# Gathered sums two chunks behind their gathers, the prompt's layer 0 finished in the value stage, and the prompt's odd mixers started with the sample's

## The chip, the core and the metric

The kernel runs on one core of a Trainium2 chip. The engines are PE (TensorE, matmuls), DVE (VectorE), ACT (ScalarE), POOL (GpSimd) and SP (SyncE, which issues most DMAs here). Each runs its own instructions in a fixed order and waits for the others by semaphores. The metric is the device time of one execution in microseconds. Before the change the median of three runs is 4570.66 us.

## What is computed

One step of a two-layer trunk on two token groups with the same weights: a prompt of 128 tokens (P) and a sample of 512 (S), of width 1024. Layer 0 mixes with a Fourier transform and a short convolution, layer 1 (the odd one) with an RG-LRU and a bidirectional RWKV-7 scan ("wkv"). After each mixer comes a PEER layer: every token picks 16 of 16384 experts in each of 8 heads, and adds their rows of a table v, weighted by the gelu of its product with their rows of a table u.

```
for l in range(DEPTH):
    sh1, sc1, g1, sh2, sc2, g2 = _modulation(cvec, P['w_mod'][l], P['b_mod'][l])
    h = _layer_norm(x) * (1.0 + sc1) + sh1
    mix = ...                                  # even or odd mixer, then w_out
    x = _layer_norm(ALPHA * x + g1 * mix, P['ln1_g'][l], P['ln1_b'][l])
    h2 = _layer_norm(x) * (1.0 + sc2) + sh2
    ffn = _peer(h2, P['peer_wq'][l], P['peer_keys'][l], P['peer_u'][l], P['peer_v'][l])
    x = _layer_norm(ALPHA * x + g2 * ffn, P['ln2_g'][l], P['ln2_b'][l])

def block(args):                               # inside _peer, by blocks of 128 tokens
    hb, ib, gb = args
    act = jax.nn.gelu(jnp.einsum('td,thkd->thk', hb, u_tab[ib]))
    return jnp.einsum('thk,thkd->td', gb * act, v_tab[ib])
```

## The kernel before

Tokens stand in tiles of 128: the prompt is one tile, the sample is four (0 to 3). The PEER layer is computed in two ways. Tiles 1 to 3 of the sample are dense: all 16384 experts are gone through in 128 chunks of 128, with hidden values from u (`hidden`, L1245), a product with scattered gates (`ge`, L1276) and a matmul with v (L1285). The prompt and tile 0 of the sample are gathered: for each of 128 slots an indirect DMA on POOL brings one row of u or v for each token (`gather`, L1145, 512 KB), and one DVE instruction of 1024 elements either takes its product with h2 (`dot`, L1138) or adds it, weighted, to a sum (`add`, L1166 and L1168). This is 4 x 128 gathers for each of the two layers, 1024 in all; "sum" stands below for either of the two DVE instructions. Names ending in P are the prompt's, in S the sample's.

The gathers are background work. A list of generators (`tasks`) yields once for each gather; `pump(n)` takes n steps, and its callers spread them: each split of a weight tile into two float32r parts pumps `rate` steps (L1225), each pair of one-hot tiles one (L1216), each chunk of the value stage a share of what is left (L1265), and in the odd mixers `pace(n, src)` pumps n steps behind a tiny POOL copy that waits for src (L222). A sum is not issued with its gather: `defer` (L212) keeps two of them back and issues the oldest. The gathered rows go to 4 buffers, and to 3 more in the value stage (`gp`, `gb`).

The stages by time in the profile: even mixers with the prompt's first PEER part to about 420 us; end of layer 0 and routing of the sample, then its gates and half of the early hidden tiles, which go to DRAM (`spill`); the value stage of layer 0 (`dense_peer`, 1023 to 1881), the last norm of the sample's tiles (to 1951); the odd mixers (`odd_mixers`, to 2940); the end of layer 1 (`end`, to 3103); routing heads (to 3415), gates and early hidden tiles (to 3643); the value stage of layer 1 (3643 to 4507) and the last norm.

In layer 0, 88 steps of the prompt's value sum are left over from the value stage (`OVER`, L1375). They run at the start of the odd mixers, paced by the sample's projections. The prompt's own odd mixer waits for them (`while B.tasks`, L1495), then for `peer_out`, and then joins the sample's. The odd mixers' body is `run` (L1378): 16 wkv units of the sample and 4 of the prompt, at most 5 at a time, each a generator, with the RG-LRU beside them; its program order follows from how the generators take turns.

The order in which each engine executes is set when the program is built: the tile framework takes instructions by program order and readiness, so it may move an instruction ahead of one that waits; `issue_after(ins)` keeps the instructions inside it behind ins on its engine. On the chip each engine's order is fixed.

## Time and profile before

| | us |
|---|---|
| median of 3 runs (lowest, highest) | 4570.66 (4562.15, 4586.86) |
| the profiled execution | 4558.22 |
| its span | 4556.4 |
| PE busy | 3837.5 (84%) |
| DVE busy | 3467.4 (76%) |
| POOL busy | 1387.9 (30%) |
| DMA, mean over the span | 263 GB/s |

The shares are means over stages with different limits, so each stage is read by itself: which engine, or DMA, is busy throughout, and what ends the waits of the others. DMA has a mean of 263 GB/s but moves over 340 in several stages and under 130 in others.

### The profile page before, as it was taken

How to read it: one execution, taken by the hardware profiler on the slowest of the kernel's cores; microseconds unless marked ns; L12 is line 12 of the kernel's file. 1: busy time of each engine (PE TensorE's matmuls, PEld its weight loads, DVE VectorE, ACT ScalarE, POOL GpSimd, SP SyncE). 2: the span in 40 equal slices, each digit the busy share in tenths (PEclk: the TensorE clock that was granted, in tenths of full speed). 3: DMA queues.
4: the chain of work that ended last, by engine and by line, in shares of the span. 5: the costliest groups of instructions: out<-in, count | busy, mean ns of one | idle time of the engine just before them, and what ended most of it. 6: DMA issues, size and time to landing. Idle time of an engine off the chain costs nothing. (4 is left out here: it accounts for less than half of the span.)

```text
span 4556.4 us, 71571 instructions
## 1 busy us (share of the span) xinstructions
PE 3837.5 (84%) x26326; PEld 3142.3 (69%) x26326; DVE 3467.4 (76%) x7480; ACT 1757.4 (39%) x3391; POOL 1387.9 (30%) x1105
## 2 busy tenths in 40 slices
PE   7977968999888999778889877719779888988897
PEld 4653767997766788634665654508779877877786
DVE  3398999987889744668554786589999787888845
ACT  2211235763322333244575543203357623332332
POOL 0044322434556200044000232253125354466300
PEclk9997989999999999887888877759999999999999
DMA  9699856999999755368531566487569999999853
GB/s 342 227 350 356 264 196 236 349 357 355 360 360 362 280 175 172 128 237 286 177 101 58 182 222 205 169 289 248 171 225 341 346 367 342 346 365 369 310 170 120
DMA packets 455551, 1198.05 MB, mean 263 GB/s; under 512 B 52848, under 2 KB 195312, under 8 KB 452128
## 3 DMA queue, kind: packets, MB, share of 16 engines
q1 hardware_dynamic: 307744, 656.54, 41.4%
q0 software_dynamic: 147456, 536.94, 32.8%
q8 instruction: 207, 3.39, 0.3%
q14 instruction: 144, 1.18, 0.1%
HBM read 1093.34 MB, written 99.98 MB: 262 GB/s over the span
## 5 line engine op out<-in xcount | busy, mean ns | idle before, releaser
L1079 PE MATMUL ps<-hiS,lwS 128*128 128x384 f32 (+1 forms) x2304 | 817.5, 356 | 81.2 <-DVE lwS L1224 80.9
L1079 PE MATMUL ps<-loS,uhS 128*128 128x384 f32 (+1 forms) x2432 | 857.9, 353 | 1.1 <-DVE loS L432 1.1
L1079 PE MATMUL ps<-hiS,uhS 128*128 128x384 f32 (+1 forms) x2304 | 813.2, 353 | 51.3 <-ACT geS L1252 26.0
L1079 PEld LDWEIGHTS ps<-hiS,lwS 128*128 128x128 f32 x2304 | 447.2, 194 | 111.7 <-DVE lwS L1224 101.4
L1222 ACT ACTIVATE uhS<-w 128x1024 fp32r<-128x1024 f32 x304 | 320.8, 1055 | 527.3 <-PE ps L1079 358.6
L1285 PE MATMUL ps<-vh,ah 128*128 128x512 f32 x1536 | 429.4, 401 | 99.9 <-ACT vh L1222 78.8
L1152 POOL DMA_INDIRECT g<-v,idxP x256 | 351.7, 1374 | 515.8 <-DVE h2P L1168 311.9
L1152 POOL DMA_INDIRECT g<-u,idxS x256 | 349.0, 1363 | 512.9 <-DVE g L1138 391.9
L1079 PEld LDWEIGHTS ps<-hiS,uhS 128*128 128x128 f32 x2304 | 447.5, 194 | 82.3 <-ACT uhS L1222 34.1
L1285 PE MATMUL ps<-lwS,ah 128*128 128x512 f32 x1536 | 483.4, 396 | 10.9 <-DVE lwS L1224 10.8
L1079 PEld LDWEIGHTS ps<-loS,uhS 128*128 128x128 f32 x2432 | 471.5, 194 | 24.0 <-DVE loS L432 3.7
L1285 PE MATMUL ps<-vh,al 128*128 128x512 f32 x1536 | 477.3, 393 | 0.0
L1224 DVE TENSOR_TENSOR lwS<-w,uhS 128x1024 fp32r<-128x1024 f32 x304 | 369.7, 1217 | 122.9 <-ACT uhS L1222 82.0
L1152 POOL DMA_INDIRECT g<-v,idxS x256 | 367.8, 1437 | 237.6 <-DVE h2S L1168 178.6
L1224 DVE TENSOR_TENSOR lwS<-w,vh 128x1024 fp32r<-128x1024 f32 x256 | 312.9, 1223 | 153.7 <-issue 79.3
L1152 POOL DMA_INDIRECT g<-u,idxP x256 | 291.7, 1139 | 414.2 <-DVE g L1138 183.2
L1285 PEld LDWEIGHTS ps<-vh,ah 128*128 128x128 f32 x1536 | 289.1, 192 | 167.1 <-ACT vh L1222 92.5
L1278 ACT ACTIVATE ah<-geS 128x384 fp32r<-128x384 f32 x256 | 134.3, 525 | 671.4 <-PE ps L1285 598.9
L1138 DVE SCALAR_TENSOR_TENSOR g<-g,h2P 128x1024 f32<-128x1024 f32 x256 | 310.2, 1216 | 81.4 <-DMA g<-u,idxP 81.0
L1168 DVE SCALAR_TENSOR_TENSOR h2P<-g,wtP,h2P 128x1024 f32<-128x1024 f32 x254 | 324.6, 1278 | 50.7 <-DMA g<-v,idxP 49.2
L1285 PEld LDWEIGHTS ps<-lwS,ah 128*128 128x128 f32 x1536 | 291.2, 191 | 81.6 <-DVE lwS L1224 20.1
L1285 PEld LDWEIGHTS ps<-vh,al 128*128 128x128 f32 x1536 | 291.4, 190 | 62.8
(480 smaller groups left out, 6687.9 us busy)
## 6 DMA issues: line engine op xcount, KB each, us to landing
w<-ut SPq DMA_DIRECT2D x256, 512.0 KB
w<-v SPq DMA_DIRECT2D x256, 512.0 KB
w<-wblk SPq DMA_DIRECT2D x142, 512.0 KB
w<-wmod SPq DMA_DIRECT2D x96, 512.0 KB
gt<-G SPq DMA_DIRECT2D x64, 768.0 KB
w<-wout SPq DMA_DIRECT2D x56, 512.0 KB
ged<-geS SPq DMA_DIRECT2D x128, 192.0 KB
G<-fa SPq DMA_DIRECT2D x12, 2048.0 KB
```

The lines of the kernel that those rows point to most:

```text
L1079: self.nc.tensor.matmul(out, a[:, s], b[:, k, :], start=k == 0 and i == 0, stop=k == 7 and i == 2)
L1138: self.nc.vector.scalar_tensor_tensor(u, u, 1.0, self.h2[t], OP.mult, OP.mult, accum_out=self.act[t][:, s:s + 1])
L1152: self.nc.gpsimd.indirect_dma_start(out=g, out_offset=None, in_=self.I[tab], in_offset=bass.IndirectOffsetOnAxis(ap=self.idx[t][:, s:s + 1 ...
L1168: nc.vector.scalar_tensor_tensor(acc, v, w[:, s:s + 1], acc, OP.mult, OP.add)
L1222: self.nc.scalar.activation(h, raw, AF.Copy)
L1224: self.nc.vector.tensor_tensor(lo, raw, h.bitcast(F32), op=OP.subtract)
L1278: nc.scalar.activation(ah, ge, AF.Copy)
L1285: nc.tensor.matmul(outs[n][h], a[:, s], b[:, 512 * h:512 * h + 512], start=c == 0 and i == 0, stop=c == 127 and i == 2)
```

## The change

- `defer` keeps back `lag` sums: 2 as before, 5 in the value stages. There the sums of the gathers of one chunk are issued two chunks later, behind that chunk's `al` on DVE (`use_gathered(fresh, i)`).
- In the value stages the gathers of a chunk are issued by `pace` on `ge`: behind a POOL copy that waits for that chunk's gate product. A chunk takes ceil(left / (122 - c)) steps, but at least 2. There are 4 more gather buffers instead of 3, and one more buffer for weight tiles.
- `OVER` is gone. The prompt's value sum and its `peer_out` of layer 0 come first among the tasks, ahead of the sample's, and all is done within the value stage. `rate` in the route is 1 instead of 2.
- The prompt's odd mixer starts at once: `odd_lora`, its RG-LRU and its projections (`wkv_inputs`, now with more turns) take part in `run` from the first turn, and its four wkv units come after the sample's first ones. The pace in the odd mixers is 3 throughout.
- Layer 1's end is new code, `end_tiles`: all four remaining weight tiles of w_out are loaded first, the matmuls of all four token tiles are issued, and then residual, norms and transposes go tile by tile instead of pair by pair.

```diff
@@ -155,7 +155,7 @@
         self.gp, self.gb, self.gn, self.wb, self.wn, self.rp = None, 0, 0, 0, 0, None
-        self.odd, self.tasks, self.pending, self.left = False, [], [], 0
+        self.odd, self.tasks, self.pending, self.left, self.lag = False, [], [], 0, 2
         self.load_constants()
@@ -211,16 +211,16 @@
         self.pending.append(use)
-        self.use_gathered(2)
-
-    def use_gathered(self, left=0):
-        while len(self.pending) > left:
-            f, *a = self.pending.pop(0)
-            with self.later(0):
+        self.use_gathered(self.lag)
+
+    def use_gathered(self, left=0, after=None):
+        with self.tc.issue_after(after.ins) if after else nullcontext():
+            while len(self.pending) > left:
+                f, *a = self.pending.pop(0)
                 f(*a)
...
     def pace(self, n, src):
-        if self.tasks:
+        if n and self.tasks:
             p = self.tl([128, 1], "pace", 2)
@@ -374,13 +374,13 @@
 
-    def row_of(self, src):
-        o = self.B.wide("row", 3)
+    def row_of(self, src, bufs=3):
+        o = self.B.wide("row", bufs)
         self.nc.sync.dma_start(o, src.broadcast_to([128, D]))
...
 
-    def mrow(self, l, v):
-        return self.row_of(self.B.md[l, v][self.row:self.row + 1, :])
+    def mrow(self, l, v, bufs=3):
+        return self.row_of(self.B.md[l, v][self.row:self.row + 1, :], bufs)
 
@@ -504,6 +504,48 @@
         self.todo.append((grp, pts))
+
+    def end_tiles(self, l, hT, lo):
+        nc, B = self.nc, self.B
+        ws = []
+        for k in range(self.early, 8):
+            w = B.rp.tile([128, D], F32, name=B.name("wo"), tag="wo", bufs=8 - self.early)
+            nc.sync.dma_start(w, self.I["wout"][l, k])
+            ws.append(w)
+        self.end_load(l)
+        xs = []
+        for t in range(self.nt):
+            x = self.tmp()
+            nc.sync.dma_start(x, self.x[t])
+            xs.append(x)
+            if t == 1:
+                break
+        g1 = self.mrow(l, 2, 5)
+        g, b = self.row_of(self.I["lnaff"][l, 0:1], 5), self.row_of(self.I["lnaff"][l, 1:2], 5)
+        mc = self.mcols(l, 3)
+        self.h2, self.todo, pts = {}, None, []
+        for t in range(self.nt):
+            pts.append([self.pst(*(("pB", 2) if t == 3 else ())) for _ in range(2)])
+            for k in range(self.early, 8):
+                for h in range(2):
+                    nc.tensor.matmul(pts[t][h], self.yT[:, k, t * 128:(t + 1) * 128],
+                                     ws[k - self.early][:, 512 * h:512 * h + 512], start=k == self.early, stop=k == 7)
+        for t in range(self.nt):
+            if t < len(xs):
+                x = xs[t]
+            else:
+                x = self.tmp()
+                nc.sync.dma_start(x, self.x[t])
+            self.residual(x, pts[t], g1, 1.0)
+            self.norm([x], g, b)
+            self.save(t, x)
+            self.norm([x])
+            self.transposed([x], (t,), mc, hT, lo)
+            if t not in self.dense:
+                sh2, sc2 = self.mrow(l, 3, 5), self.mrow(l, 4, 5)
+                h2 = self.h2[t] = self.keep([128, D], "h2")
+                nc.vector.scalar_tensor_tensor(h2, sc2, 1.0, x, OP.add, OP.mult)
+                nc.vector.tensor_tensor(h2, h2, sh2, op=OP.add)
 
@@ -616,6 +658,7 @@
             lo.append(o)
+            yield
         nc.scalar.activation(lo[0], lo[0], AF.Tanh)
@@ -733,6 +776,8 @@
                     self.shift(z[:, hp, :], z[:, hp, 1:T + 1], 4 * i + hp)
+                    if hp < 3:
+                        yield
                 rkv.append([z[:, 0:2, 1:T + 1], z[:, 2:4, 1:T + 1]])
@@ -1257,12 +1302,10 @@
         f.update(zip(self.dense, outs))
+        self.B.lag, fresh = 5, 0
         for c in range(128):
...
                 self.B.finish_task(first)
-            elif c < LAST:
-                more = self.B.left - (OVER if l < DEPTH - 1 else 0)
-                self.B.pump(max(0, -(-more // (LAST - c))))
             if 0 not in f and first not in self.B.tasks:
@@ -1276,7 +1319,14 @@
             nc.scalar.activation(ah, ge, AF.Copy)
-            nc.vector.tensor_tensor(al, ge, ah.bitcast(F32), op=OP.subtract)
+            i = nc.vector.tensor_tensor(al, ge, ah.bitcast(F32), op=OP.subtract)
+            if self.B.lag > 2:
+                self.B.use_gathered(fresh, i)
+            had = len(self.B.pending)
+            if c < LAST:
+                more = self.B.left
+                self.B.pace(min(more, max(2, -(-more // (LAST - c)))), ge)
+            fresh = max(0, len(self.B.pending) - had)
             vh, vl = self.split(self.dt, "vh", self.I["v"][l * NEXP + c * 128:l * NEXP + (c + 1) * 128])
@@ -1327,20 +1377,24 @@
             with B.tc.tile_pool(name=f"ends{l}", bufs=1, reuse_waits="tile") as B.rp:
-                self.end(l, self.hi, self.lo, l == 0 and (lambda: B.modulation(1, 0)))
+                if self.early:
+                    self.end_tiles(l, self.hi, self.lo)
+                else:
+                    self.end(l, self.hi, self.lo, l == 0 and (lambda: B.modulation(1, 0)))
             B.rp = None
...
                 self.peer_tiles(l)
-                B.rate = 2
+                B.rate = 1
+                if l == 0:
+                    B.add(P.values(0))
+                    B.add(P.peer_out(0), n=1)
                 for h in self.route(l, self.groups[0]):
...
                 B.add(self.dots(0, range(128)), mine, n=256)
-                if l == 0:
-                    B.add(P.values(0))
                 self.spilled = {}
@@ -1354,10 +1408,10 @@
             with B.tc.tile_pool(name=f"dense{l}", bufs=1, reuse_waits="tile") as self.dense_pool:
-                B.gp, B.gb, B.rp = self.dense_pool, 3, self.dense_pool
+                B.gp, B.gb, B.wb, B.rp = self.dense_pool, 4, 1, self.dense_pool
                 B.rate, f = 0, {}
                 self.dense_peer(l, G, ges, mine, f)
-                B.gp, B.gb = None, 0
+                B.gp, B.gb, B.wb, B.lag = None, 0, 0, 2
                 for grp in (((1, 2), (3,)), ((1,), (2,), (3,)), ((1,), (2, 3)))[1]:
@@ -1372,7 +1426,7 @@
 SPILL = 16
-LAST, OVER = 122, 88
+LAST = 122
 
@@ -1492,16 +1546,11 @@
     def prompt(own, side):
-        while B.tasks:
-            yield
-        for _ in range(4):
-            yield
-        yield from P.peer_out(l - 1)
-        B.odd_rate = 3
-        P.odd_lora(l)
+        yield from P.odd_lora(l)
         lru, wkv = [P.odd_lru(l, c) for c in range(4)], list(P.odd_wkv(l))
...
         side[n:n] = lru
+        yield from P.wkv_inputs(l, P.inputs, 0)
         own.extend(wkv)
@@ -1517,9 +1566,10 @@
 
-    B.odd, B.odd_rate = True, 6
+    B.odd, B.odd_rate = True, 3
     B.odd_constants()
-    S.odd_lora(l)
+    for _ in S.odd_lora(l):
+        pass
     lru = [S.odd_lru(l, c) for c in range(4)]
```

How many sums (of 1024) stand on DVE in each stretch of its order, between instructions that both kernels have:

| stretch of DVE's order | before | after |
|---|---|---|
| up to the sample's first top-k of layer 0 | 78 | 78 |
| its routing heads | 74 | 67 |
| gates and early hidden tiles | 63 | 17 |
| value stage of layer 0, first to last gate product | 209 | 348 |
| then to the last wkv output | 184 | 157 |
| end of layer 1, to the sample's first top-k | 59 | 92 |
| its routing heads | 43 | 5 |
| gates and early hidden tiles | 58 | 0 |
| value stage of layer 1 and behind | 256 | 260 |

In the row that ends with the last wkv output, the 184 are 88 value sums of layer 0 and 96 dots of layer 1, the 157 are 2 value sums of the sample's tile 0, the prompt's 128 dots and 27 of its value sums. In the end of layer 1, 59 are 32 dots and 27 value sums, and the 92 are value sums alone.

Place one is POOL's order in the value stage of layer 0 (g are gathered rows, `pace` the copy that waits for a chunk's gate product `geS`). Before:

```order
L1152 DMA g_10816<-v,idxS_2899 128x1024
L1152 DMA g_10852<-v,idxS_2899 128x1024
L1152 DMA g_10855<-v,idxS_2899 128x1024
L1152 DMA g_10889<-v,idxS_2899 128x1024
L1152 DMA g_10892<-v,idxS_2899 128x1024
```

After:

```order
L1197 DMA g_11445<-u,idxS_2899 128x1024
L225 COPY pace_11515<-geS_11305 128x1
L225 COPY pace_11589<-geS_11347 128x1
L1197 DMA g_11447<-u,idxS_2899 128x1024
L1197 DMA g_11517<-u,idxS_2899 128x1024
L225 COPY pace_11661<-geS_11389 128x1
L1197 DMA g_11519<-u,idxS_2899 128x1024
```

The gathers stood in one row without a copy between them, each held only by its buffer; now they stand in groups behind a copy from the gate product.

Place two is DVE's order in the same stage (`lwS` is the low part of a split weight tile, `al` that of the gated hidden values). Before:

```order
L1279 TENSOR_TENSOR al_10862<-geS_10646,ah_10861 128x384
L1168 SCALAR_TENSOR_TENSOR h2S_8844<-g_10813,wtS_8841,h2S_8844 128x1024
L1168 SCALAR_TENSOR_TENSOR h2S_8844<-g_10816,wtS_8841,h2S_8844 128x1024
L1224 TENSOR_TENSOR lwS_10869<-w_10865,vh_10867 128x1024
L1279 TENSOR_TENSOR al_10899<-geS_10714,ah_10898 128x384
L1168 SCALAR_TENSOR_TENSOR h2S_8844<-g_10852,wtS_8841,h2S_8844 128x1024
L1276 TENSOR_TENSOR geS_10821<-geS_10821,gt_10969 128x384
L1276 TENSOR_TENSOR geS_10858<-geS_10858,gt_10969 128x384
```

After:

```order
L1269 TENSOR_TENSOR lwS_10905<-w_10901,vh_10903 128x1024
L1183 SCALAR_TENSOR_TENSOR g_10852,actS_2900<-g_10852,h2S_2756 128x1024
L1322 TENSOR_TENSOR al_10929<-geS_10724,ah_10928 128x384
L1269 TENSOR_TENSOR lwS_10947<-w_10943,vh_10945 128x1024
L1183 SCALAR_TENSOR_TENSOR g_10854,actS_2900<-g_10854,h2S_2756 128x1024
L1322 TENSOR_TENSOR al_10971<-geS_10797,ah_10970 128x384
L1183 SCALAR_TENSOR_TENSOR g_10856,actS_2900<-g_10856,h2S_2756 128x1024
L1319 TENSOR_TENSOR geS_10841<-geS_10841,gt_11009 128x384
L1269 TENSOR_TENSOR lwS_10989<-w_10985,vh_10987 128x1024
```

Sums stood wherever they fitted in; now they stand behind the `al` of a later chunk, here dots of the sample's tile 0, where the kernel before has come to its value sums.

Place three is DVE's order in the end of layer 1, in the second norm of the first token tiles (`rsS` is the norm's small state, `h2P` the prompt's sum). Before:

```order
L1138 SCALAR_TENSOR_TENSOR g_26917,actP_21590<-g_26917,h2P_21528 128x1024
L401 TENSOR_SCALAR rsS_26525<-mvS_26524 128x2
L402 TENSOR_SCALAR rsS_26525<-rsS_26525 128x2
L403 TENSOR_SCALAR rsS_26525<-rsS_26525 128x2
L405 TENSOR_TENSOR rsS_26525<-rsS_26525 128x2
L1138 SCALAR_TENSOR_TENSOR g_26953,actP_21590<-g_26953,h2P_21528 128x1024
L406 SCALAR_TENSOR_TENSOR rsS_26525<-rsS_26525 128x2
L407 SCALAR_TENSOR_TENSOR rsS_26525<-rsS_26525 128x2
L405 TENSOR_TENSOR rsS_26525<-rsS_26525 128x2
L406 SCALAR_TENSOR_TENSOR rsS_26525<-rsS_26525 128x2
```

After:

```order
L1213 SCALAR_TENSOR_TENSOR h2P_27566<-g_30048,wtP_27563,h2P_27566 128x1024
L405 TENSOR_TENSOR rsS_26746<-rsS_26746 128x1
L405 TENSOR_TENSOR rsS_26826<-rsS_26826 128x1
L1213 SCALAR_TENSOR_TENSOR h2P_27566<-g_30109,wtP_27563,h2P_27566 128x1024
L406 SCALAR_TENSOR_TENSOR rsS_26746<-rsS_26746 128x1
L406 SCALAR_TENSOR_TENSOR rsS_26826<-rsS_26826 128x1
L1213 SCALAR_TENSOR_TENSOR h2P_27566<-g_30136,wtP_27563,h2P_27566 128x1024
L407 SCALAR_TENSOR_TENSOR rsS_26746<-rsS_26746 128x1
L407 SCALAR_TENSOR_TENSOR rsS_26826<-rsS_26826 128x1
L1213 SCALAR_TENSOR_TENSOR h2P_27566<-g_30158,wtP_27563,h2P_27566 128x1024
```

Before, one dot stands between nine small steps; now a value sum stands between each small step and the next, two tiles' steps being paired.

## Rows read from the trace of the kernel before

**Rows 1.** Busy time of each engine by stage: window, length, busy (instructions), granted clock, DMA.
```profile
core 0: us, PE busy (x) PEld busy (x) DVE busy (x) ACT busy (x) POOL busy (x), PEclk, DMA share, GB/s
1023.00:1881.00 858.00, 783.93 (x3658) 670.29 (x3659) 607.94 (x726) 274.58 (x371) 282.81 (x204) 0.98 0.80 286
3643.00:4507.00 864.00, 789.23 (x3634) 683.38 (x3635) 659.21 (x857) 272.18 (x365) 355.02 (x252) 0.96 0.87 312
...
2940.00:3103.00 163.00, 60.11 (x199) 36.14 (x198) 125.83 (x223) 21.14 (x40) 80.73 (x67) 0.67 0.84 289
3103.00:3415.00 312.00, 264.04 (x1391) 239.53 (x1390) 308.80 (x1117) 133.73 (x272) 56.99 (x44) 0.94 0.61 206
...
3415.00:3643.00 228.00, 216.75 (x1429) 216.17 (x1427) 192.57 (x169) 163.16 (x404) 102.67 (x59) 0.99 0.94 344
```

**Rows 2.** The same view of three stretches of the value stages.
```profile
1202.00:1530.00 328.00, 269.42 (x1204) 220.79 (x1203) 289.75 (x317) 88.85 (x120) 194.64 (x140) 0.97 0.98 361
1585.00:1785.00 200.00, 200.00 (x973) 176.19 (x972) 94.13 (x117) 73.90 (x101) 0.00 (x0) 1.00 0.55 177
3880.00:3981.00 101.00, 100.01 (x484) 87.82 (x483) 84.42 (x125) 36.26 (x50) 41.90 (x35) 1.00 0.97 348
```

**Rows 3.** The same stretches, the gate product (L1276, one a chunk) alone.
```profile
1202.00:1530.00 328.00, 21.70 (x40) 0.97 0.98 361
1585.00:1785.00 200.00, 17.62 (x32) 1.00 0.55 177
3880.00:3981.00 101.00, 8.89 (x16) 1.00 0.97 348
```

**Rows 4.** The page's DMA queue of the gathers: packets, MB, share of 16 engines.
```profile
q0 software_dynamic: 147456, 536.94, 32.8%
```

**Rows 5.** Busy time of each engine in six stretches of the odd stage.
```profile
1951.00:2029.00 78.00, 63.59 (x158) 28.79 (x156) 55.61 (x78) 29.95 (x54) 41.49 (x41) 0.94 0.80 277
2029.00:2114.00 85.00, 66.96 (x906) 38.23 (x906) 76.40 (x161) 54.27 (x105) 37.09 (x36) 0.76 0.78 258
2114.00:2228.00 114.00, 82.66 (x1163) 61.61 (x1162) 84.14 (x211) 41.96 (x96) 31.10 (x28) 0.66 0.71 243
2228.00:2536.00 308.00, 270.18 (x4403) 193.11 (x4406) 161.56 (x534) 205.23 (x452) 0.67 (x4) 0.85 0.31 97
2536.00:2839.00 303.00, 240.26 (x3329) 168.26 (x3320) 235.70 (x721) 125.71 (x269) 90.38 (x112) 0.77 0.63 212
2839.00:2940.00 101.00, 82.33 (x1359) 65.89 (x1360) 62.32 (x206) 26.03 (x67) 20.82 (x28) 0.67 0.42 143
```

**Rows 6.** Groups of DVE in 1068:1537: busy us, mean ns; idle before, releaser.
```profile
L1168 DVE SCALAR_TENSOR_TENSOR h2S<-g,wtS,h2S 128x1024 f32<-128x1024 f32 x127 | 162.8, 1282 | 1.8
L1224 DVE TENSOR_TENSOR lwS<-w,vh 128x1024 fp32r<-128x1024 f32 x62 | 75.5, 1220 | 6.2 <-ACT vh L1222 6.2
...
L1279 DVE TENSOR_TENSOR al<-geS,ah 128x384 fp32r<-128x384 f32 x62 | 34.2, 552 | 9.6 <-ACT ah L1278 9.6
```

**Rows 7.** All gathers (L1152): time from issue to landing.
```profile
DMA to landing us min/median/max: 4.1/7.3/14.6
```

**Rows 8.** Waits in 1068:1537: who waited for whom, total us, times, longest.
```profile
POOL g L1152 <- DVE h2S L1168: 96.7, 75, 8.3
```

**Rows 9.** The POOL copies of L225 from the odd units, ns min/median/max.
```profile
L225 POOL COPY pace<-e x12: 181/619/1102, 2037.1 to 2853.4; 128x1 f32<-128x1 f32 x12
```

**Rows 10.** Waits in 2550:2930: who waited for whom.
```profile
DVE g L1138 <- DMA g<-u,idxP: 53.9, 35, 8.3
```

**Rows 11.** Groups of DVE in 2940:3103, the end of layer 1.
```profile
L1138 DVE SCALAR_TENSOR_TENSOR g<-g,h2P 128x1024 f32<-128x1024 f32 x32 | 38.8, 1214 | 9.5 <-DMA g<-u,idxP 9.3
L1168 DVE SCALAR_TENSOR_TENSOR h2P<-g,wtP,h2P 128x1024 f32<-128x1024 f32 x26 | 33.4, 1284 | 8.9 <-DMA g<-v,idxP 8.7
...
L552 DVE TENSOR_TENSOR half<-ps,row 128x512 f32<-128x512 f32 x8 | 5.4, 682 | 17.5 <-DMA w<-wout 17.5
```

## The prediction

> **What bounds the kernel now.** I read the stages first, by the busy time of the engines in each [rows 1], then the inside of each stage. The two value stages (layer 0 from 1023 to 1881 us, layer 1 from 3643 to 4507) have two regimes, shown by three stretches [rows 2], in which the gate product, once a chunk, counts the chunks [rows 3]. In 1202:1530 there are 40 chunks in 328 us and 140 gathers (all of POOL's instructions there), the DMA engines are 0.98 busy at 361 GB/s, and PE idles. In 1585:1785 there are 32 chunks in 200 us and no gather, PE is busy throughout and DMA moves 177 GB/s. In 3880:3981 there are 16 chunks in 101 us with 35 gathers: PE is busy throughout and DMA moves 348 GB/s. So a chunk costs PE 6.25 us (200/32) and DMA 1.106 MB (177 GB/s x 200 us / 32), and a gather 0.524 MB (537 MB over the program's 1024 [rows 4]). Three and a half gathers a chunk need (1.106 + 3.5 x 0.524) / 0.361 = 8.15 us of DMA, and 8.2 was measured; two need 5.97 us, less than PE wants. **Two gathers a chunk are free, each further one costs 1.45 us.** DVE comes close behind: in the DMA-bound regime it works for 290 of 328 us.
>
> The odd stage (1951 to 2940) is read in six stretches [rows 5]. [...] In 2228:2536, with no sum, PE is busy for 270 of 308 us at 0.85. The last two stretches hold 96 of the prompt's dots. Layer 1's end up to the first top-k of the sample (2940:3103) belongs to DVE, 126 of 163 us, while PE works for 60. The routing heads behind it (3103:3415) are DVE's alone, 309 of 312 us. The gates and early hidden tiles (3415:3643) are PE's, 217 of 228 us [rows 1].
>
> **The change part by part**, against the profiled execution (4558 us, span 4556). Where the sums stand in DVE's order is the table ahead of this.
>
> Value stage of layer 0. It now takes 348 sums where it had 209: the 88 that were left to the odd stage, and those that one pump instead of two for each split leaves behind in the route. The pace gives three gathers a chunk while more than two are left for each remaining chunk, so 106 chunks with three, 16 with two, 6 with none. 106 x (1.106 + 3 x 0.524) / 0.361 = 787 us, 22 x 6.25 = 138, together 924 us against 858: **+66**. Lower bound: all bytes at the ceiling without a gap, (128 x 1.106 + 348 x 0.524) / 0.361 = 897, +39. Upper bound: three gathers cost what 3.5 cost in the row, 8.2 us, 106 x 8.2 + 138 = 1007, +149. I stand by the first, since bytes explain both regimes. DVE needs 3 x 1.28 for the sums, 1.22 for v's split, half of that for u's (half of the tiles come from the spill), 0.55 twice [rows 6]: 6.8 us of 7.4, so it follows, with little to spare. The sum stands two chunks (14.8 us) behind its gather, which lands within 14.6 us at worst, 7.3 by the median [rows 7]; eight buffers and the issue of three gathers hold this, and POOL's present waits for a sum to free a buffer [rows 8] move to the pace. The prompt's last norm, inside the stage, is covered by DMA.
>
> A pace copy reads SBUF on POOL while DVE's sums read two SBUF operands. The row of such copies gives 181, 619 and 1102 ns as least, median and largest [rows 9], so some wait for something; POOL, with 3 gathers in 7.4 us, has room for that. [...]
>
> Value stage of layer 1. 258 sums at nearly two a chunk: 14 chunks with three, 14 x 7.42 = 104 us, and 114 at 101/16 = 6.31, 720 us; 824 against 864: **-41**. Bounds: 128 x 6.25 = 800 (-64), and no change (0) if the spacing costs what the idle DMA of its last 222 us gave.
>
> Routing heads. DVE-bound, so a sum taken out is worth its time: in layer 1 the count falls from 43 to 5, 38 x 1.27 = 48, less a little because PE's own 264 us come near: **-45** (-48 to -30). In layer 0 it falls by 7: **-8**. The sums that leave the gates' stretch (58 and 46) lay under a PE that was 95% busy: 0, and they now cost where they land.
>
> Odd stage. Without its 88 sums the first 277 us could run as 2228:2536 does: 213 us of PE at 270/308 are 243, -34; and 83 us of it at 0.85 instead of 0.66 are 64, -19. That includes the prompt's projections, which move ahead of the first units. Together -55 (0 to -90). The late part gets 155 sums where it has 96, because the prompt's dots end earlier and 27 value sums follow them before the last units are out. 59 x 1.28 = 76 us of DVE work, and by now the dots' own waits for their gathers take 54 us [rows 10]. Against that, the prompt's top-k starts after the 11th of 20 units instead of the 14th: three units more of cover, 3 x 33 us (308 us for 9 units) at a DVE that is idle for 48%, 48 us, and the stretch itself has another 20 us or so. I take +10 (-20 to +110, that is the 76 plus 59 x 0.56 of waits). Sum **-45** (-110 to +55).
>
> End of layer 1. 92 sums stand between its steps, where 59 did (58 of them in the window of [rows 11]), one after nearly every small operation of the norms. DVE's work: 126 - 39 - 33 = 54 for the end itself, 92 x 1.28 = 118 for the sums. The wait of 17.5 us at its start [rows 11] remains, with 7 sums (9 us) in it. 54 + 118 + 8.5 = 180 against 163, +17 with no wait for a gather; with the present 0.31 us for each sum (9.3 + 8.7 over 58) 209, +46. The tiles' own pipeline (all four weights first, tile by tile on DVE) gives something back: **+33** (+15 to +60).
>
> Tails. The last gathers are now summed in the last chunks, so tile 0 is finished behind them instead of far earlier: four half-row steps and two of statistics at 0.68 us [rows 11], two at 1.28 and some small ones, 8 to 9 us of DVE, half of it beside the last chunks' matmuls: **+4** for each layer, +8 (0 to +17).
>
> Sum: 66 - 41 - 45 - 8 - 45 + 33 + 8 = -32: 4526 us in the profile's terms.
>
> **Rivals.** (a) The odd stage packs densely: once no sum stands in its first half, PE stays near the 88% of the free stretch to the end and the clock stays up. Odd stage -110 instead of -45, end +17: 4526 - 65 - 16 = 4445. For it: clock and busy share rise together in the rows. Against: 155 sums in its second half. [...] (b) Slower: the value stage of layer 0 saturates both DMA and DVE. DVE executes in order; if a sum's gather is late even by half a microsecond at 361 GB/s, the split behind it is late, PE waits, and the next pace with it. Then a chunk with three gathers costs the 8.2 us of [rows 2]: +149 instead of +66, 4609. It decides from about 7.7 us a chunk, where 106 x 0.3 = 32 us have eaten the gain. For it: DVE at 6.8 of 7.4 us. Against: in the DMA-bound regime DVE waited for gathers hardly at all (1.8 us beside 127 sums [rows 6]). (c) Four buffers feed the 92 and 27 sums around layer 1's end, and DVE stands behind each: odd stage -10, end +60, 4526 + 35 + 27 = 4588. (d) The pacing doesn't do what it says: layer 1's value stage keeps its 864 us, 4567.
>
> **How the numbers follow.** A measurement of this kernel can tell about 0.5% (23 us) from no change. Forecast 0.42 (own range 4490 to 4560, so 0.26 faster and 0.16 within); (a) 0.25, faster; (b) 0.18, slower; (c) 0.11, slower; (d) 0.04, within. That makes faster 0.51, within 0.20, slower 0.29. The median of the runs shown, 4570.66, lies 0.27% above the profiled execution, 12 us: 4526 becomes 4538. The range takes in (a) with most of its spread and (b) likewise: 4425 to 4640; outside stay an odd stage at its lower bound with everything else well, and (b) together with (c). The signs share the cases: the forecast's own range is 4502 to 4572.
>
> **What would show it.** Right: layer 0's value stage 900 to 940 us long with DMA near 360 GB/s to its last chunks; layer 1's 810 to 835 with PE busy nearly throughout; a first wkv unit without sums around it and a clock over 0.8 in the odd stage's first half; an end of layer 1 of 180 to 210 us; heads of layer 1 in some 265 us. Wrong: DVE waits for gathers in the value stages, layer 0 over 960 us, or an odd stage as long as before (989 us) because its second half has become DVE's.

## The result

The changed kernel takes 4501.1 us (median of 4 runs, 4496.9 to 4510.8) against 4572.2 us of the kernel before in the same session (4562.2 to 4586.9): a ratio of 0.9845 with a 95% interval of 0.9813 to 0.9877, 71 us faster. The forecast was 4538, and faster; the range held the time, but the gain is twice the one forecast.

Of the 71 us the two traces show 55 (spans 4556 and 4501 us); the other 16 are the profiled executions, of which that of before was a quick one (4558 beside a median of 4572) and that of after was not. By the markers that the prediction used (first and last gate product, first and last unit, first top-k), in us:

| stage | before | after | change | forecast |
|---|---|---|---|---|
| start to first sample top-k, layer 0 | 456 | 460 | +4 | 0 |
| routing heads, layer 0 | 348 | 338 | -10 | -8 |
| gates, layer 0 | 219 | 216 | -3 | 0 |
| **value stage, layer 0** | 854 | 894 | **+40** | +66 |
| last gate product to 11th unit | 547 | 466 | **-81** | -55 +4 |
| 11th unit to last wkv output | 516 | 570 | **+54** | +10 |
| end of layer 1 | 162 | 215 | **+53** | +33 |
| routing heads, layer 1 | 312 | 262 | -50 | -45 |
| gates, layer 1 | 228 | 236 | +8 | 0 |
| **value stage, layer 1** | 864 | 797 | **-66** | -41 |
| last chunk to the end | 46 | 43 | -3 | +4 |

The busy time by stage of the kernel after answers [rows 1]; the columns are those of [rows 1].

```profile
core 0: us, PE busy (x) PEld busy (x) DVE busy (x) ACT busy (x) POOL busy (x), PEclk, DMA share, GB/s
1014.00:1908.00 894.00, 794.79 (x3654) 681.77 (x3655) 765.59 (x951) 272.26 (x371) 560.87 (x470) 0.96 0.98 360
3657.00:4454.00 797.00, 764.38 (x3644) 668.92 (x3645) 646.43 (x842) 272.48 (x369) 453.41 (x380) 0.98 0.96 344
2943.00:3159.00 216.00, 62.33 (x195) 38.73 (x196) 171.67 (x291) 24.89 (x65) 117.72 (x93) 0.62 0.82 280
3159.00:3421.00 262.00, 238.85 (x1326) 219.36 (x1325) 260.08 (x1078) 127.99 (x265) 3.75 (x4) 0.98 0.48 160
3421.00:3657.00 236.00, 228.66 (x1500) 228.28 (x1498) 122.97 (x109) 166.44 (x408) 0.00 (x0) 0.99 0.57 201
```

The value stage of layer 1 is now PE's, 764 of 797 us. In the end of layer 1 (2943:3159) DVE works 172 us where it worked 126, beside a PE that is no busier than it was. The gates of layer 1 behind the heads (3421:3657) have no POOL instruction left, and DMA falls from 0.94 to 0.57: room that nobody uses. Inside the value stages, two stretches answer [rows 2], and the gate products in them (L1319 now) answer [rows 3]:

```profile
1304.00:1760.00 456.00, 412.39 (x1909) 353.77 (x1907) 399.05 (x533) 139.53 (x190) 313.40 (x258) 0.97 1.00 373
3872.00:4169.00 297.00, 297.00 (x1439) 262.10 (x1438) 241.78 (x326) 105.71 (x144) 162.19 (x139) 1.00 0.95 341
...
1304.00:1760.00 456.00, 35.12 (x65) 0.97 1.00 373
3872.00:4169.00 297.00, 26.57 (x49) 1.00 0.95 341
```

The windows begin and end with a gate product, so that 65 of them are 64 chunks. In layer 0 these take 456 us, 7.1 us each, with 193 gathers and DMA at 1.00 and 373 GB/s, which is more than the 361 of [rows 2]. In layer 1, 48 chunks take 297 us, 6.2 each, with 93 gathers and PE busy throughout.

Just ahead of the first of these stretches stands the prompt's last norm of layer 0. Its eight chunks took 79 us with 24 gathers, where other groups of eight with 22 to 26 gathers took 52 to 60, and DMA fell to 309 GB/s. The second line is from the waits in 1225:1760: POOL's copy waited for gate products, once for 27.2 us. In every kernel below in which the prompt ends early, the group with this norm is the longest of layer 0, 74 to 134 us. No run took the norm out of the stage.

```profile
1225.00:1304.00 79.00, 59.80 (x257) 49.16 (x256) 67.28 (x109) 22.16 (x31) 38.45 (x32) 0.87 0.86 309
...
POOL pace L225 <- DVE geS L1319: 37.5, 12, 27.2
```

The odd stage in three stretches (before: [rows 5]): no gather in the first, 139 POOL instructions in the second, and a clock of 0.54 in the last, where PE works for 72 of 125 us.

```profile
2047.00:2374.00 327.00, 286.71 (x4779) 198.72 (x4778) 175.33 (x570) 217.54 (x485) 0.00 (x0) 0.86 0.36 113
2374.00:2818.00 444.00, 364.22 (x4990) 250.33 (x4988) 350.50 (x1070) 202.19 (x428) 126.93 (x139) 0.79 0.61 202
2818.00:2943.00 125.00, 71.60 (x1281) 57.82 (x1280) 84.83 (x163) 27.22 (x64) 58.44 (x56) 0.54 0.68 228
```

### The profile page after: what moved, and what is told of

It is laid out like the page before. It is cut to its first block, busy times and chain, and to the rows that moved or that the text cites. A ratio compares the mean times of both kernels' runs of the same rounds, so it can differ in the third digit from the quotient of the medians.

```text
span 4501.2 us, 72085 instructions
## 1 busy us (share of the span) xinstructions
PE 3794.0 (84%) x26326; PEld 3122.6 (69%) x26326; DVE 3463.1 (77%) x7548; ACT 1749.2 (39%) x3413; POOL 1534.8 (34%) x1317
## 5 line engine op out<-in xcount | busy, mean ns | idle before, releaser
L1124 PE MATMUL ps<-hiS,lwS 128*128 128x384 f32 (+1 forms) x2304 | 807.8, 352 | 53.0 <-DVE lwS L1269 52.7
L1335 PE MATMUL ps<-vh,ah 128*128 128x512 f32 x1536 | 411.0, 397 | 66.9 <-ACT vh L1267 59.3
L1197 POOL DMA_INDIRECT g<-v,idxS x256 | 385.1, 1504 | 238.6 <-DVE h2S L1213 192.2
L1197 POOL DMA_INDIRECT g<-v,idxP x256 | 337.7, 1319 | 359.8 <-DVE h2P L1213 194.7
L225 POOL COPY pace<-geS 128x1 f32<-128x1 f32 x244 | 149.2, 616 | 748.4 <-DVE geS L1319 704.0
```

The costliest lines, as they stand in the source:

```text
L225: self.pump(n, self.nc.gpsimd.tensor_copy(p, src[:, 0:1]))
L1124: self.nc.tensor.matmul(out, a[:, s], b[:, k, :], start=k == 0 and i == 0, stop=k == 7 and i == 2)
L1197: self.nc.gpsimd.indirect_dma_start(out=g, out_offset=None, in_=self.I[tab], in_offset=bass.IndirectOffsetOnAxis(ap=self.idx[t][:, s:s + 1 ...
L1335: nc.tensor.matmul(outs[n][h], a[:, s], b[:, 512 * h:512 * h + 512], start=c == 0 and i == 0, stop=c == 127 and i == 2)
```

## The experiments

The change is three things at once: how gathers and sums are handed out in the value stages (distance, pace, buffers), the prompt's early end of layer 0, and the new end of layer 1. My theory after the two traces: the first part carries the gain, because sums five behind and held in place make the gathers even, and the prompt's early end loses on one side (end of layer 1, layer 0's value stage) what it brings on the other. The rivals: the gain comes from the odd stage being clear, or within the first part from the buffers or the pace alone. Stages in the table are in us, by the markers above; odd is from the last gate product to the last wkv output.

| kernel | median, ratio to before (95%) | value 0 | odd | end 1 | heads 1 | gates 1 | value 1 |
|---|---|---|---|---|---|---|---|
| before | 4572 | 854 | 1063 | 162 | 312 | 228 | 864 |
| after | 4501, 0.9845 (0.9813 to 0.9877) | 894 | 1035 | 215 | 262 | 236 | 797 |
| value stages alone | 4490, 0.9817 (0.9792 to 0.9841) | 823 | 1072 | 165 | 318 | 215 | 812 |
| after, old buffers | 4538, 0.9916 (0.9888 to 0.9944) | 924 | 1035 | 216 | 262 | 235 | 806 |
| after, two behind | 4506, 0.9850 (0.9824 to 0.9875) | 896 | 1037 | 217 | 263 | 241 | 790 |
| after, no pace | 4495, 0.9827 (0.9802 to 0.9852) | 887 | 1031 | 217 | 267 | 238 | 787 |
| after, pace only | 4541, 0.9922 (0.9894 to 0.9950) | 929 | 1037 | 216 | 263 | 240 | 793 |
| after, neither holds | 4583, 1.0021 (1.0006 to 1.0035) | 894 | 1055 | 212 | 333 | 215 | 801 |
| after, four a chunk | 4596, 1.0053 (1.0034 to 1.0071) | 925 | 1033 | 212 | 262 | 237 | 859 |
| values held | **4415**, 0.9650 (0.9621 to 0.9680) | 896 | 1011 | 99 | 331 | 227 | 794 |
| held, old end | 4433, 0.9687 (0.9662 to 0.9711) | 894 | 1006 | 114 | 334 | 228 | 786 |
| held, value stages alone | 4492, 0.9818 (0.9800 to 0.9837) | 818 | 1072 | 120 | 345 | 233 | 824 |
| held in both layers | 4418, 0.9650 (0.9619 to 0.9680) | 889 | 995 | 100 | 331 | 233 | 803 |
| held, two in gates | **4370**, 0.9551 (0.9528 to 0.9573) | 848 | 1014 | 100 | 331 | 234 | 790 |

### The value stages alone

The kernel before with the new hand-over (from defer's lag to pace on ge, fourth gather buffer, wide buffer); everything else old. Of its diff, the hand-over and the buffers:

```diff
-            elif c < LAST:
-                more = self.B.left - (OVER if l < DEPTH - 1 else 0)
-                self.B.pump(max(0, -(-more // (LAST - c))))
...
+            if c < LAST:
+                more = max(0, self.B.left - (OVER if l < DEPTH - 1 else 0))
+                if more:
+                    self.B.pace(min(more, max(2, -(-more // (LAST - c)))), ge)
...
-                B.gp, B.gb, B.rp = self.dense_pool, 3, self.dense_pool
+                B.gp, B.gb, B.wb, B.rp = self.dense_pool, 4, 1, self.dense_pool
```

> The kernel before with the new way of handing out gathers in the value stages alone: sums queued five behind and placed behind the rounding error, the POOL copy that waits for ge, a fourth gather buffer and a wide one. 88 gathers of the prompt are still held back, the prompt still ends layer 0 inside the odd stage, and end, odd stage and routing rate are those of before. Theory A, that this part carries the gain and that the early prompt costs about what it gives back: the value stage of layer 1 falls from 864 to about 798 us as in the changed kernel, that of layer 0, which has 139 sums fewer than the changed kernel's 348, falls from 854 to about 800, and heads, odd stage and the end of layer 1 stay within 10 us of before; 4572 - 66 - 54 is about 4450, faster than the changed kernel's 4501. Theory B, that the gain comes from the order as a whole (the prompt's last work out of the odd stage) and that the value stage of layer 0 gains nothing without it: about 4572 - 66, 4505.

4490 us. Layer 1's stage gained 52 and layer 0's 31, not 54; no other stage moved by more than 13. This part alone gives 82 us, no less than the whole change (the two intervals overlap), so the early prompt and the new end together gave nothing that can be measured, as they stand. Theory A is right in its claim, 40 us too hopeful in its sum.

### Distance, pace, buffers

> The changed kernel with three extra gather buffers and no extra wide one in the value stages, as before. Theory A, that the gain of the value stages rests on sums that stand far enough behind their gathers, and that six gathers open at a time need the buffers: a gather waits for the buffer of the sum it follows, and the two value stages lose 20 to 60 us together, 4521 to 4561. Theory B, that the pace and the place of the sums are enough: within 10 us of 4501.

```diff
-                B.gp, B.gb, B.wb, B.rp = self.dense_pool, 4, 1, self.dense_pool
+                B.gp, B.gb, B.wb, B.rp = self.dense_pool, 3, 0, self.dense_pool
```

4538, theory A's figure: 30 us of it in layer 0's stage, 8 in layer 1's. Its reason, that five queued sums need the buffers, is put to the test by the run with the pace alone.

> The changed kernel with sums queued two behind their gathers in the value stages, as before, and not placed behind the rounding error; the POOL copy that waits for ge, the buffers and all else are the changed kernel's. Theory A, that DVE's wait for a gather's rows is what the stage of layer 1 lost before, and that the distance takes it away: the stage of layer 1 goes back from 798 us to 850 or more and that of layer 0 from 894 to 940 or more, 4600 in all. Theory B, that the even pace alone takes it away: within 15 us of 4501.

```diff
-        self.B.lag, fresh = 5, 0
+        self.B.lag, fresh = 2, 0
```

4506, theory B: the distance that gave the change its name, and the place behind `al` that the kernel uses only with it, are worth nothing that can be measured while the pace is there.

> The changed kernel without the POOL copy that waits for ge in the value stages: gathers are handed out in the same numbers, at least two per chunk, but nothing ties their issue to the chunk. Sums stay five behind, and the buffers are the new ones. Theory A, after the run in which sums stood only two behind and the time stayed at 4506: the pace is what the value stages gain from, and without it both lose what they had gained, value stage of layer 1 from 798 to about 850 us, of layer 0 from 894 to about 940, 4600 in all. Theory B, that any of the three (pace, distance, buffers) is enough where the other two stay: within 15 us of 4501.

```diff
-                self.B.pace(min(more, max(2, -(-more // (LAST - c)))), ge)
+                self.B.pump(min(more, max(2, -(-more // (LAST - c)))))
```

4495, theory B again: neither is the pace, while the distance is there. The stages are 7 and 10 us shorter without its copies, which the intervals of the two kernels don't tell apart.

> The changed kernel with sums two behind and the gather buffers of before in the value stages, so that only the pace is left of that part. Its order has 64 sums of layer 1's dots in heads and gates, 58 less in the value stage. Theory A, that buffers count only because five queued sums hold them (the run with the old buffers and five behind lost 30 us in layer 0's value stage and 8 in layer 1's): with two behind they are enough, 4501 within 15 us. Theory B, that fewer buffers cost by themselves, because gathers land late: 4530 to 4560.

```diff
-        self.B.lag, fresh = 5, 0
+        self.B.lag, fresh = 2, 0
...
-                B.gp, B.gb, B.wb, B.rp = self.dense_pool, 4, 1, self.dense_pool
+                B.gp, B.gb, B.wb, B.rp = self.dense_pool, 3, 0, self.dense_pool
```

The order that this text speaks of is not that of this kernel; its heads and gates have 7 and 0 sums, where the changed kernel's have 5 and 0. 4541, theory B for layer 0, where the fewer buffers cost 35 us with two sums queued, as they cost 30 with five; in layer 1 nothing is lost (793). This kernel's whole stage and its middle, windows and gate products as in [rows 2] and [rows 3], beside the 894 and 456 us above:

```profile
1011.00:1940.00 929.00, 809.63 (x3640) 686.23 (x3641) 770.73 (x967) 272.36 (x369) 571.41 (x470) 0.95 0.94 345
1303.00:1789.00 486.00, 422.09 (x1916) 358.43 (x1915) 407.62 (x539) 139.65 (x190) 329.28 (x266) 0.96 0.97 357
...
1303.00:1789.00 486.00, 34.53 (x64) 0.96 0.97 357
```

Here the windows' ends fall just outside two gate products, and 64 chunks take 486 us. Six gathers more (199 for 193) are by estimate some 8 of the 30 us, at 0.524 MB each [rows 4] and 373 GB/s; the rest is DMA, which moves 357 GB/s where it moved 373. Over the whole stage, with the same 348 gathers, it is 345 for 360. Where three gathers a chunk make DMA the bound, these buffers are bandwidth. The gather buffer and the one for weight tiles were always taken away together, so which of them counts is not shown.

So buffers explain that loss in layer 0, and the gain in layer 1 survived the loss of each of the three. What is left is what all these kernels share. Counted per eight chunks of layer 1 in the traces (gathers issued, us), first group to last:

```
before      us  31 57 76 53 50 50 50 61 65 65 65 57 50 50 50 35
       gathers   8 28 29 17 17 16 17 29 28 28 28  7  0  0  0  0
after       us  50 58 57 50 50 50 50 48 51 49 49 51 50 48 51 38
       gathers  18 23 21 15 16 16 16 16 15 13 18 17 13 18 17  6
```

The last group ends with the last gate product and is seven chunks. Eight chunks take 50 us with 0 gathers and with 16, 57 with 23, 65 with 28 (57 and 76 in the two groups of the first pack, 67 on average). Before, gathers ran ahead of the chunk that handed them out, in two packs at 28, and the last four groups had none. Two runs put this to the test, each able to fail.

> The changed kernel with one number changed: at least four gathers handed out per chunk in the value stages for at least two; pace, distance and buffers are the changed kernel's. In its order the value stage of layer 1 has 21 to 25 sums in each of ten groups of eight chunks and then hardly any, where the changed kernel has 16 in nearly all. Theory A, that evenness is what the value stage of layer 1 gained: eight chunks take 50 us with up to 16 gathers, 57 with 24 (the changed kernel's groups in layer 0), 65 with 28 (before), so 798 us becomes about 850, layer 0 stays within 15 us of 894, and the whole takes about 4555. Theory B, that the stage's time goes by the sum of gathers, however they lie, or by the waits that distance and buffers took away: within 15 us of 4501.

```diff
-                self.B.pace(min(more, max(2, -(-more // (LAST - c)))), ge)
+                self.B.pace(min(more, max(4, -(-more // (LAST - c)))), ge)
```

Theory A in layer 1: 859 us for the stage, with distance, pace and buffers in place; 4596 in all, half a per cent slower than before the change, where theory A had 4555. The trace has 18 to 25 gathers in each of the first eleven groups of layer 1, about three a chunk, then 2, then none. The windows of a stretch with gathers and of the one behind it, without, and their gate products:

```profile
3731.00:4133.00 402.00, 364.05 (x1669) 314.82 (x1669) 349.52 (x493) 121.92 (x166) 259.68 (x222) 0.96 1.01 375
4358.00:4507.00 149.00, 149.00 (x723) 131.57 (x722) 69.29 (x85) 54.28 (x72) 0.00 (x0) 1.00 0.53 175
...
3731.00:4133.00 402.00, 30.86 (x57) 0.96 1.01 375
4358.00:4507.00 149.00, 13.25 (x25) 1.00 0.53 175
```

First 56 chunks at 7.2 us with DMA full and PE waiting, then 24 at 6.2 with DMA half idle: what the first stretch loses, the second can't give back, since PE has its own floor. Layer 0 lost 31 us too, which theory A had not said: its pack of 67 gathers in the fourth group, where the prompt's last norm stands, took 134 us, and the last two groups had none.

> The changed kernel without either of the two things that tie gathers to the chunk (the POOL copy that waits for ge, and sums placed behind the rounding error, five behind); the new buffers and the numbers handed out stay. Alone, each of the two could be taken out at no cost (4495 and 4506 us). In the order 64 sums of layer 1's dots move ahead into its heads (58 sums for 5) and gates (13 for 0), and its value stage has 24 in each of four groups of eight chunks and none in the last five. Theory A, that either of the two is enough to keep gathers where they are handed out, and that without both they run ahead: heads 262 to about 335, value stage 798 to about 815, 4580 in all. Theory B, that the buffers carry the gain: 4501 within 15 us.

```diff
-        self.B.lag, fresh = 5, 0
+        self.B.lag, fresh = 2, 0
...
-                self.B.pace(min(more, max(2, -(-more // (LAST - c)))), ge)
+                self.B.pump(min(more, max(2, -(-more // (LAST - c)))))
```

Theory A: 4583. Without both, heads and gates hold 66 sums more and the value stage 64 fewer; it is no shorter (801, with PE busy for 764), for PE's floor of 6.2 us a chunk is there, and the heads pay 71 us for 53 sums. With the gates, which are 21 us shorter, that is 50 us for 66 sums; another 20 lie in the odd stage, which holds as many sums as it did (155 for 157), and why it is longer no run shows. The heads' window and the stage's:

```profile
3175.00:3508.00 333.00, 279.21 (x1480) 254.75 (x1479) 330.28 (x1189) 136.94 (x278) 76.02 (x59) 0.94 0.66 226
3723.00:4525.00 802.00, 764.01 (x3635) 665.57 (x3636) 592.95 (x735) 272.26 (x367) 248.11 (x186) 0.99 0.83 296
```

DVE is busy for 330 of the 333 us of the heads. So the pace, and the sums placed behind the rounding error, are two locks on one door: either keeps the gathers where the chunk hands them out.

### The sums in the end of layer 1

The end of layer 1 was the largest loss. Its groups on DVE and who DVE waited for, in the kernel after (before: [rows 11]):

```profile
L1213 DVE SCALAR_TENSOR_TENSOR h2P<-g,wtP,h2P 128x1024 f32<-128x1024 f32 x93 | 119.3, 1283 | 37.4 <-DMA g<-v,idxP 37.2
...
L594 DVE TENSOR_TENSOR half<-ps,row 128x512 f32<-128x512 f32 x8 | 5.4, 682 | 6.6 <-DMA row<-md 6.6
```

93 value sums for 119 us, and 37 us of waits for their gathers, in a stage of 216.

> The changed kernel with one line changed: in layer 1 the hand-over of one gather per weight tile in the routing goes through a small POOL copy that reads that tile, so that the 92 value sums of the prompt that now stand in the end of layer 1 (3 are left there) fall into its heads (51) and gates (61, none before). Theory A, that the end of layer 1 grew from 162 to 215 us because these sums and their gathers stand between its few DVE instructions, and that the gates, where TensorE is busy 229 of 236 us, take them free: end 216 to about 115, heads 262 to about 310 (before had 43 sums there and took 312), gates 236 to 240, 4501 - 50, about 4450. Theory B, that the end is held by its own chain and by its loads, and the sums only fill its waits: end 216 to about 200, heads plus 50, 4530.

```diff
-        self.B.pump(self.B.rate)
+        (self.B.pace if self.B.odd else lambda n, _: self.B.pump(n))(self.B.rate, raw)
```

Theory A, and more of it than I had asked for: 4415. The windows of the end, the heads, the gates:

```profile
2920.00:3020.00 100.00, 60.59 (x200) 38.85 (x201) 64.51 (x205) 25.99 (x68) 4.97 (x8) 0.76 0.38 137
3020.00:3350.00 330.00, 266.93 (x1383) 242.07 (x1383) 317.82 (x1126) 131.85 (x269) 83.85 (x94) 0.90 0.60 208
3350.00:3578.00 228.00, 218.08 (x1437) 217.50 (x1435) 193.10 (x168) 161.42 (x402) 115.37 (x99) 0.99 0.93 345
```

The end falls by 116 us and the odd stage's tail, behind the start of its last unit, by 26 (19 sums there for 49); the heads take 46 sums more and 69 us; the gates take 61 sums at hardly any cost, DMA from 0.57 to 0.93, PE as busy as it was. Some 60 matmuls moved from the gates' window to the heads', so the gates' 228 us for 236 are no gain: 0.159 us a matmul for 0.157, 2 us in all.

> The changed kernel with the end of layer 1 as before the change (tile by tile with the old loads) and the gathers of layer 1's routing held by the POOL copy; 11 sums are left in that end, for 92 in the changed kernel and 3 in the held one, whose time was 4415. Theory A, that the new end is what shortened the end of layer 1 to 100 us once the sums had gone: with the old one it takes 130 to 150, 4445 to 4465. Theory B, that the sums alone did it: within 15 us of 4415.

On top of the held kernel:

```diff
-                if self.early:
-                    self.end_tiles(l, self.hi, self.lo)
-                else:
+                if 1:
```

Between the two: 4433, end 114 for 99. So the new end is worth 18 us at most. The intervals of the two kernels overlap, and the old end holds 8 sums more (11 for 3), which at 1.28 us each would be 10 of its 15. What the new end is worth beside 92 sums, no run shows.

> The kernel of the first run (the new hand-over in the value stages alone, the prompt still ending layer 0 in the odd stage, 4490 us) with the gathers of layer 1's routing held by the POOL copy. Its order has 16 sums in the end of layer 1 for 57, 65 in the heads for 47, 63 in the gates for 56. Theory A, that sums in the end of layer 1 cost 1.2 us and more each whichever way the prompt goes: end 165 to about 115, heads 318 to about 335, 4490 - 35, about 4455; the early prompt is then worth some 40 us, as the kernel that has both took 4415. Theory B, that the end of layer 1 is long here for its own order of work and not for the sums: end 165 to about 155, 4490 within 15 us; the changed end is then worth the difference.

On top of the value stages alone:

```diff
-        self.B.pump(self.B.rate)
+        (self.B.pace if self.B.odd else lambda n, _: self.B.pump(n))(self.B.rate, raw)
```

Theory B by the time, 4492 for 4490, but not by its reason. The end did fall by 45 us; the gates already had 56 sums there, so the sums went to heads, gates and value stage (18, 7 and 16 more), and these took 27, 18 and 12 us more. The windows of its end and gates:

```profile
2914.00:3034.00 120.00, 57.62 (x199) 37.22 (x198) 75.26 (x162) 19.49 (x38) 25.50 (x31) 0.73 0.58 203
3379.00:3612.00 233.00, 223.73 (x1445) 222.09 (x1443) 195.59 (x170) 161.06 (x402) 128.97 (x100) 0.99 0.91 335
```

With the values held, the early prompt and the new end are worth 4492 - 4415 = 77 us; without, 4490 and 4501 can't be told apart. The table says where: the early prompt's price is paid in layer 0's value stage (896 for 818), and its return comes in the odd stage (1011 for 1072), the end (99 for 120), the heads and gates (558 for 578) and layer 1's value stage (794 for 824). The change lost this return in its end, which took 215 us.

### Gates of layer 0

> The kernel that holds the gathers of layer 1's routing (4415 us), with those of layer 0's routing held in the same way: 37 sums for 78 ahead of the first sample top-k, 63 for 67 in the heads, 62 for 17 in the gates, 348 in the value stage of both. Theory A, that gates take sums free in layer 0 too and that the end of layer 0 in front of the first top-k loses about 1 us for each of 41 sums: 460 to about 420, 4375 in all. Theory B, that the stretch ahead of the first top-k waits for its loads and TensorE, and the sums stand in its gaps: 4415 within 15 us.

On top of the held kernel, as the run behind this one:

```diff
-        (self.B.pace if self.B.odd else lambda n, _: self.B.pump(n))(self.B.rate, raw)
+        self.B.pace(self.B.rate, raw)
```

4418, theory B by the time, but not by its reason: the start gained 27 us (433 for 460), and heads and gates lost 12 and 24.

> The kernel that holds the gathers of layer 1's routing (4415 us), handing out two gathers per weight tile for one in the gates of layer 0: 59 sums there for 17, 306 in the value stage for 348, of them 46 in its third group of eight chunks and 16 in each of the last seven full ones for 24. Theory A, that sums beyond 16 per eight chunks cost about 1 us each and gates take them for less: value stage 896 to about 865, gates 216 to between 216 and 240 (the kernel that held both layers had 62 sums there and took 240), 4385 to 4410. Theory B, that in layer 0 a sum costs as much in the gates as in the value stage: 4415 within 10 us.

```diff
                 self.routing = False
+                B.rate = 2 if l == 0 else 1
                 for t in (2, 3):
```

4370, better than theory A: the gates took 42 sums more in 214 us for 216, and the value stage lost 48 us for 42 sums. The windows of the gates, of a late stretch of the value stage, and the gate products of that stretch:

```profile
802.00:1016.00 214.00, 210.90 (x1385) 209.90 (x1383) 189.73 (x165) 160.68 (x400) 96.20 (x59) 0.99 0.94 349
1579.00:1827.00 248.00, 248.00 (x1202) 218.96 (x1201) 205.52 (x221) 87.64 (x119) 161.19 (x122) 1.00 0.95 343
...
1579.00:1827.00 248.00, 22.34 (x41) 1.00 0.95 343
```

From two a chunk on, layer 0 too runs at PE's 6.2 us a chunk. This version beats both kernels, by 202 and 131 us.

## Why the prediction came out as it did

The mechanism of the value stages was right (two gathers a chunk free, 50 us for eight chunks with none and with 16; the further ones at DMA's price, 57 us with 23), the direction too, and only five of the eleven stages came out more than 10 us from their term. The price in bold was too high: 1.45 us is DMA's time for one gather (0.524 MB at 361 GB/s), but a chunk with three costs 7.42 - 6.25 = 1.17 us above PE's floor by the figures that the sums used, and 0.9 as measured (7.1 for 6.2). The steps that failed:

- **Value stage of layer 0, +66, came out +40.** The term divided bytes by 0.361 MB/us as DMA's ceiling. That was the rate of a stretch with seven gather buffers, and the change adds one, and a wide one, which I listed only as cover for the distance. With 373 GB/s from the window above the same sum is 106 x 2.68 / 0.373 + 138 = 899 us, +41. With the old buffers the stage took 924 and 929, and 924 was my sum. That these sums meet the stage so closely is in part luck, since what they leave out nearly cancels: the prompt's last norm, which I had as covered by DMA, cost some 20 us (79 for its group, 52 to 60 for others with 22 to 26 gathers), while the first and the last group, with 13 and 6 gathers, took 38 and 37 us for 57 and 50. The copies on POOL, for which the sum has no term, cost little: without them the stages are 7 and 10 us shorter, within the spread of the two kernels.
- **Value stage of layer 1, -41, came out -66**, near the bound I gave for PE alone (-64). The groups with three gathers were sized rightly (165 us for the first three, 167 by my prices); the last group, seven chunks up to the last gate product, took 38 us and not 50, and the rest ran at 6.2 a chunk and not 6.31.
- **The odd stage's two halves, -55 and +10, came out -81 and +54.** The first half did what rival (a) said, and its clock in 2047:2374 is 0.86. The 213 us of PE in the first half's term are those of the first three stretches in [rows 5], and its 0.66 and 0.85 the granted clocks of 2114:2228 and 2228:2536 there. The second half didn't: I let three more units cover the 59 added sums for 68 of their 76 us. Little was covered. From the 11th to the 20th unit the stretch grew by 30 us with 30 sums more (106 for 76), and behind the 20th by 24 us with 29 more (49 for 20). The held kernel bears out the second: with 19 sums its tail took 99 us, where the kernels with 49 or 50 took 118 to 125, which is 0.6 to 0.9 us a sum.
- **End of layer 1, +33, came out +53**, inside its bounds and near rival (c). DVE's own work (52 us) and its sums (119) are as forecast; the step that failed is the wait for gathers, 0.40 us for each sum (37.2 / 93), where [rows 11] had 0.31 and I took half. That these sums need not stand there at all, I did not see: I priced where the order put them, and never what it would cost to hold them.
- **Rivals.** (b) did not come: DVE follows at 7.1 us a chunk. (d) is wrong in its time, though its doubt had a point: pacing and distance are each dispensable, evenness is not. The ground given for (a), that clock and busy share rise together, holds in part of the rows only: in [rows 5] 1951:2029 has a clock of 0.94 and 2839:2940 one of 0.67, each with PE busy for 82% of it.

Together: the value stages gave 51 us more than forecast, the odd stage and the end 34 less, the rest 5 more, and 16 lie between the profiled executions: the 39 us, to a rounding, between -32 and -71. The prediction put the median 12 us above the profiled execution, as before the change; behind it the median, 4501.1, lies 2 us below the profiled 4502.9.

What stays open is why layer 0's gates lost 24 us with 62 sums in the run that held both layers and none with 59 in the last one. The traces of these gates show a difference: where both were held, DVE waited 25 us for gathers, whose POOL copies had waited 70 us for weight tiles; in the last run it waited 4. Waits in 782:1021 of the first, then in 802:1016 of the last:

```profile
DVE g L1183 <- DMA g<-u,idxP: 18.8, 7, 5.0
DVE h2P L1213 <- DMA g<-v,idxP: 6.6, 3, 4.5
POOL pace L225 <- DMA w<-ut: 70.0, 18, 13.6
...
DVE h2P L1213 <- DMA g<-v,idxP: 3.8, 2, 2.2
```

That these waits are the loss was not tested, and layer 1's gates bore the same copies, which waited 20 us there, without one.

## What to carry to other kernels

A stage with two bounds (here PE at 6.2 us a chunk, and DMA, for which each gather beyond two added 1.0 to 1.25 us in the groups above) was shortest with the extra load spread evenly (797 us for layer 1's value stage, 859 with at least four gathers handed out a chunk); a pack costs the time above the floor, and the empty stretch behind it gave nothing back (24 chunks at 6.2 us without a gather). A scheduler that may run loads ahead can make packs, as it did here, so tie each load to the step that is to carry it, by one wait. Before pricing where moved work lands, look for the stage with an idle resource (here the gates, DMA at 0.57) and hold the work back for it: that was worth 86 us on top of the change, which gave 71.

## What the runs showed of the hardware

The rate of mixed gathers and weight loads rose with the buffers: in the middle of layer 0's value stage 357 GB/s at a share of 0.97 without the two new ones, 373 at 1.00 with them (345 and 360 over the whole stage), and 375 in layer 1 with a pack. So the "full" DMA of [rows 2], 361 GB/s at 0.98, was not full. And 61 gathers with their sums went into the gates of layer 1 almost without lengthening them, while DMA went from 201 to 345 GB/s beside a PE that was busy for 218 of 228 us.
